# Taking GpSimd arithmetic out of the mixers and merges, and reordering the first expert search, in a two-layer hybrid network

## The chip, the cores and the metric

One core of one Trainium2 chip runs the whole network in one launch. The metric is the time of one execution on the device in microseconds. The engines are TensorE (PE; its weight loads are PEld), VectorE (DVE), ScalarE (ACT), GpSimd (POOL) and SyncE (SP). They run side by side, and each works through its own queue of instructions in order.

## The reference, cut to what matters

Two layers act on 512 latent rows (`x_lat`) and 256 context rows (`x_ctx`) of width 1024:

```python
for l in range(DEPTH):
    h_lat = rmsnorm(x_lat, norm1_g[l]) * (1.0 + sc1) + sh1          # same for h_ctx
    ys = ssm_mixer(...)      # two diagonal complex state-space scans (forward, backward), 16 groups
    yd = diff_mixer(...)     # differential attention, 4 heads
    yn = na_mixer(...)       # neighbourhood attention, 4 heads
    m = sigmoid(g_ssm)*(ys@w_br_ssm) + sigmoid(g_diff)*(yd@w_br_diff) + sigmoid(g_na)*(yn@w_br_na)
    x_lat = x_lat + g1 * (m @ w_out[l])
    x_lat = x_lat + g2 * peer_ffn(h2, peer_wq[l], peer_subkeys[l], peer_u[l], peer_v[l])
    # context rows: the same in layer 0, left out after the mixers' inputs in layer 1

def peer_ffn(h, ...):        # 8 heads, 128 x 128 = 16384 experts, 16 chosen for each row and head
    s = einsum(h @ wq, subkeys); sv, si = top_k(s, 16)        # twice, one for each half of the key
    best, pos = top_k(sv0[:, None] + sv1[None, :], 16); eidx = ...
    act = gelu(einsum(u_tab[eidx], h)); return einsum(softmax(best) * act, v_tab[eidx])
```

All is fp32; the kernel splits the operands of its large products into a high and a low part (`hi`, `lo`) and sums three products.

## The kernel before, in words

`run` calls `layer` twice. A layer has three stages.

`front`: the inputs are normalised (`start`, in layer 0), then three streams are woven together: `mixers` (projections and attention), `states` (`ssm_prep` and `ssm`) and `gates`. `ssm_prep` computes the tables of the state-space scans: complex powers, the matrices `sbt`, `scb` and the rotations `rot`. In layer 0 it runs beside `start`; the tables of layer 1 are prepared at the end of layer 0's `states`. `ssm` scans two groups at a time. All complex products go through `cmul` (L236): four instructions on VectorE, and on GpSimd the product at L243 and, unless `neg` is set, the sum at L247.

`merge` (L926) runs for the context rows and for the latent rows in layer 0, for the latent rows in layer 1. For each of 8 slices of 128 columns it takes three products, weighs each with its gate on VectorE (L946), sums the three on GpSimd (L947, L948), and splits the sum into `mh` and `ml` (ScalarE L61, VectorE L62). Then the output product, times a gate on VectorE (L968), is added to the rows on GpSimd (L969). In layer 0 `modulation` for layer 1 is woven in beside it; both stream weights through a ring of three `raw` buffers.

The expert stage: `own` rows (the context rows in layer 0, 128 latent rows in layer 1) are computed by gathering the chosen rows of `u` and `v`; the others by running all experts densely. `routing` holds in layer 0: `chosen` for the context rows (the search: queries, scores, `top16`), `route` for each of the two tiles (which writes the row numbers, `picks`), then the search and routes of the latent rows (`rest`), woven with `counted` at 1.0 to 0.9. `counted` steps through `gathered`: one indirect DMA of 128 rows on GpSimd's queue (L1200, five ahead) and one VectorE instruction (L1214 or L1222). `early` is 128 dense units: each splits a block of 512 KB and takes 24 products with the 512 latent rows. After both, `experts` takes the second dense product, with what is left of the gathers beside it.

What sets the order is `weave` (L123): a stream yields a cost for each step, and the stream with the smallest share of its total goes next. The totals are written out by hand. The framework then places the instructions on each engine's queue, and can move one ahead of another where the data allow it. All loads and most stores go through SP's queue.

Of the kernel before, what the change touches and what calls it, by code (L numbers as in the profile page):

```python
# [50 lines left out]
class Net:  # L51
# [87 lines left out]
    def drain(g):  # L139
        for _ in g:  # L140
            pass

    @contextmanager
    def psum(self, **banks):

        with ExitStack() as es:
            self.banks = {k: n if isinstance(n, str) else es.enter_context(
                self.tc.tile_pool(name=k, bufs=n, space=PSUM, reuse_waits="tile")) for k, n in banks.items()}
            yield
# [85 lines left out]

    def cmul(self, o, x, y, t, neg=False):  # L236

        v, g = self.nc.vector, self.nc.gpsimd
        v.tensor_mul(o[0], x[0], y[0])
        v.tensor_mul(t, x[1], y[1])  # L240
        v.tensor_sub(o[0], o[0], t)
        v.tensor_mul(t, x[0], y[1])
        g.tensor_mul(o[1], x[1], y[0])  # L243
        if neg:
            v.scalar_tensor_tensor(o[1], o[1], -1.0, t, op0=ALU.mult, op1=ALU.subtract)
        else:
            g.tensor_add(o[1], o[1], t)  # L247

    def exps(self, x, p, name, shape):

# [675 lines left out]
    def merge(self, l, x, t0, n, p):  # L926

        nc, v = self.nc, self.nc.vector
        ts = slice(t0, t0 + n)
        yh, yl, mh, ml = [p.tile([128, 8, n], F32R, name=a, bufs=1) for a in ("yh", "yl", "mh", "ml")]  # L930
        for k in range(8):
            t = p.tile([128, n], F32, name="yt")
            self.dma(t, self.ybuf[l][k, :, ts])
            self.split(t, yh[:, k], yl[:, k])
            yield 0.50
        for j in range(4):
            w = self.wchunk(self.a["w_br"][l, j])
            for h in range(2):
                c = slice(128 * h, 128 * h + 128)
                g = p.tile([128, 3, n], F32, name="g3")  # L940
                self.dma(g, self.gbuf[l][2 * j + h, :, :, ts])
                for b, (k0, nk) in enumerate(((0, 2), (2, 4), (6, 2))):
                    ps = self.ps1("mg")
                    self.mm3(ps[:, :n], lambda k: (w[0][:, k0 + k, c], w[1][:, k0 + k, c]),
                             lambda k: (yh[:, k0 + k], yl[:, k0 + k]), nk)
                    v.scalar_tensor_tensor(g[:, b], g[:, b], 1.0, ps[:, :n], op0=ALU.add, op1=ALU.mult)  # L946
                nc.gpsimd.tensor_add(g[:, 0], g[:, 0], g[:, 1])  # L947
                nc.gpsimd.tensor_add(g[:, 0], g[:, 0], g[:, 2])  # L948
                self.split(g[:, 0], mh[:, 2 * j + h], ml[:, 2 * j + h])
            yield 5.00  # L950
        tiles = range(t0 // 128, (t0 + n) // 128)
        gate = {}
        for r in sorted({1 if i < 2 else 0 for i in tiles}):
            gate[r] = p.tile([128, D], F32, name=f"g1{r}", bufs=1)
            self.dma(gate[r], self.arow[l][r:r + 1, 2 * D:3 * D].to_broadcast([128, D]))
        xt = {}
        for i in tiles:
            xt[i] = p.tile([128, D], F32, name=f"x{i - tiles[0]}", bufs=1)
            self.dma(xt[i], x[i])
        for j in range(4):  # L960
            w = self.wchunk(self.a["w_out"][l, j])
            c = slice(256 * j, 256 * j + 256)
            for i in reversed(tiles):
                t = slice(128 * i - t0, 128 * i - t0 + 128)
                ps = self.ps1("mg")
                self.mm3(ps[:, :256], lambda k: (mh[:, k, t], ml[:, k, t]), lambda k: (w[0][:, k], w[1][:, k]), 8)
                d = p.tile([128, 256], F32, name="d")
                v.scalar_tensor_tensor(d, ps[:, :256], 0.5, gate[1 if i < 2 else 0][:, c], op0=ALU.mult, op1=ALU.mult)  # L968
                nc.gpsimd.tensor_add(xt[i][:, c], xt[i][:, c], d)  # L969
            yield 4.00  # L970
        for i in reversed(tiles):
            self.dma(self.xs[i], xt[i])
# [409 lines left out]
    def layer(self, l):  # L1382
        self.front(l)
        own = (0, 1) if l == 0 else (2,)
        n = 512 if l == 0 else 384
        with self.pool("ga", 1, "right") as pa:
            rows = {i: pa.tile([128, D], F32, name=f"row{i}") for i in own}
            picks = {i: (pa.tile([128, 128], U32, name=f"pick{i}"), pa.tile([128, 128], F32, name=f"pw{i}")) for i in own}
            sums = self.gathered(l, own, rows, picks, pa)
            left = [256.0 * len(own)]  # L1390

            def counted():
                for c in sums:
                    left[0] -= c
                    yield c

            self.pace = None

            def routing():
                got = []  # L1400
                if l == 0:
                    with self.pool("route", 2) as p:
                        hc = [p.tile([128, 8, 256], F32R, name=a, bufs=1) for a in ("hch", "hcl")]
                        with self.pool("fin") as pn:
                            self.prepared(l, 0, hc, 0, rows, p, pn)
                        yield 5.0
                        yield from self.chosen(l, 0, 256, hc, got, p)
                        for i in own:
                            yield from self.route(l, *got[i], p, picks=picks[i])
                    got = []  # L1410
                with self.pool("route", 2) as p:
                    def rest():
                        if l == 0:
                            yield from self.chosen(l, 0, 512, h2, got, p)
                        for i in range(2, 6):
                            if i not in own:
                                yield from self.route(l, *got[i - 2], p, at=4 * (i - 2))

                    if l > 0:
                        yield from self.chosen(l, 0, 512, h2, got, p)  # L1420
                        for i in own:
                            yield from self.route(l, *got[i - 2], p, picks=picks[i])
                    yield from self.weave((rest(), 1.0), (counted(), GATHER[l]), lead=True)

            with self.pool("h2", 1, "right") as ph, self.stream(ROWS, 4), self.psum(mm=4, s=4), self.pool("early", 2) as pe:
                h2 = [ph.tile([128, 8, 512], F32R, name=a) for a in ("h2h", "h2l")]
                with self.pool("norm", 1) as p, self.pool("fin") as pn:
                    for i in (2, 4):
                        self.prepared(l, i, h2, 128 * (i - 2), rows, p, pn)
                self.drain(self.weave((routing(), 760.0 if l == 0 else 420.0), (self.early(l, h2, n, pe), 128.0)))  # L1430

            self.gate = {}
            late = [(i, rows[i]) for i in own]
            with self.psum(stay=n // 128), self.stream(ROWS, 2, LAST + 3), self.pool("ep", 2) as pe:
                def beside():
                    yield from counted()
                    for i in own:
                        self.finish(l, i, rows[i], rows[i])
                        yield 5.0

                def ends(x, acc):
                    i = 6 - n // 128 + x
                    to = pe.tile([128, D], F32, name=f"sum{x}", bufs=1)
                    self.finish(l, i, acc, to)
                    if l < DEPTH - 1:
                        late.append((i, to))

                        while late and (x == n // 128 - 1 or x and len(late) > 1):
                            self.renew(l, *late.pop(0))

                self.experts(l, n, pe, ends, beside(), left[0] + 5.0 * len(own))
# [103 lines left out]
```

## Time and profile before

| | |
|---|---|
| median of 3 runs | 4922.6 us (4914.19 to 4927.8) |
| profiled execution | 4922.7 us, span 4920.9 us |
| mean granted TensorE clock | 0.95 |
| busy: TensorE / VectorE / ScalarE / GpSimd | 91% / 76% / 38% / 28% |
| mixers of layer 0, then merge | to about 800 us, to about 1095 us |
| expert stage of layer 0 | about 1140 to 2900 us, the first gather at 1284.88 us |
| layer 1 | from about 2900 us |

Busy time is the time in which an engine executes something. The granted clock is the share of full speed that TensorE had in a stretch. "Idle before" names the instruction whose end let the waiting one go.

### The profile page before, as it was taken

To read this page: it belongs to the slowest core of one execution; us is meant where nothing else is said; L and a number is where in the kernel's file an instruction comes from. 1 tells how busy PE (TensorE), PEld (TensorE's weight loads), DVE (VectorE), ACT (ScalarE), POOL (GpSimd) and SP (SyncE) were. 2 spreads that over 40 slices of the span, in tenths; PEclk is the share of its full clock that TensorE was granted. 3 is DMA by queue.
4 is the path that set the end of the run, shared out by engine and by line. 5 is a ranking of instruction groups with operands and counts; after the bars stand their busy time and mean duration, and the time that the engine had idled before them with its cause. 6 is when DMAs were issued, how large, how long until landed. Compare 5 with 4: busy or idle time off the path is not lost. (4 is left out here: it accounts for less than half of the span.)

```text
span 4920.9 us, 69116 instructions
## 1 busy us (share of the span) xinstructions
PE 4470.1 (91%) x24197; PEld 3733.3 (76%) x24197; DVE 3763.9 (76%) x8444; ACT 1845.4 (38%) x3019; POOL 1371.3 (28%) x1088
## 2 busy tenths in 40 slices
PE   7898898888998899887999997999769999989998
PEld 3687776677776787666888886877669999978887
DVE  8277885646888899997878854877545799978888
ACT  3144344424322254442222223445233355533333
POOL 4000210120265445643333310000200033334552
PEclk8999899898999999998999998999889999999999
DMA  5553434754598789999999965542434489999997
GB/s 203 168 149 101 133 123 131 238 187 148 200 329 315 265 315 341 340 333 373 367 341 345 347 213 173 149 131 94 162 124 138 156 324 350 342 331 386 367 378 269
DMA packets 462839, 1215.19 MB, mean 247 GB/s; under 512 B 47690, under 2 KB 181914, under 8 KB 458906
## 3 DMA queue, kind: packets, MB, share of 16 engines
q1 hardware_dynamic: 311002, 690.61, 41.3%
q0 software_dynamic: 110592, 402.70, 22.4%
q10 hardware_dynamic: 40896, 117.46, 6.1%
q8 instruction: 190, 3.11, 0.3%
q14 instruction: 159, 1.30, 0.1%
HBM read 1031.54 MB, written 179.04 MB: 246 GB/s over the span
## 5 line engine op out<-in xcount | busy, mean ns | idle before, releaser
L1200 POOL DMA_INDIRECT grow<-in_u_rows,pick x384 | 519.5, 1353 | 1223.8 <-DVE grow L1214 381.1
L61 ACT CAST hi<-raw 128x1024 fp32r<-128x1024 f32 x490 | 512.4, 1051 | 899.6 <-PE s L71 589.7
L62 DVE TENSOR_TENSOR lo<-raw,hi 128x1024 fp32r<-128x1024 f32 x490 | 606.6, 1241 | 314.2 <-ACT hi L61 307.6
L72 PE MATMUL s<-h2h,lo 128*128 128x512 f32 (+1 forms) x2048 | 764.7, 374 | 62.0 <-DVE lo L62 61.7
L1200 POOL DMA_INDIRECT grow<-in_v_rows,pick x384 | 608.2, 1584 | 695.5 <-PE stay L1271 236.2
L70 PE MATMUL s<-h2h,hi 128*128 128x512 f32 (+1 forms) x2048 | 773.0, 378 | 12.9 <-ACT eact L1238 8.3
L71 PE MATMUL s<-h2l,hi 128*128 128x512 f32 (+1 forms) x2048 | 761.2, 372 | 0.2 <-DVE h2l L62 0.2
L1268 PE MATMUL stay<-hiv,wh 128*128 128x512 f32 x1792 | 708.5, 396 | 46.9 <-ACT hiv L61 46.9
L1269 PE MATMUL stay<-lov,wh 128*128 128x512 f32 x1792 | 708.4, 395 | 0.0
L1271 PE MATMUL stay<-hiv,wl 128*128 128x512 f32 x1792 | 562.6, 395 | 0.0
L1222 DVE SCALAR_TENSOR_TENSOR row<-grow,gw,row 128x1024 f32<-128x1024 f32 x381 | 488.0, 1281 | 94.3 <-DMA grow<-in_v_rows,pick 91.6
L1214 DVE SCALAR_TENSOR_TENSOR grow<-grow,row 128x1024 f32<-128x1024 f32 x384 | 463.2, 1220 | 98.3 <-DMA grow<-in_u_rows,pick 97.7
L72 PEld LDWEIGHTS s<-h2h,lo 128*128 128x128 f32 x2048 | 391.7, 191 | 121.4 <-DVE lo L62 76.3
L61 ACT CAST wh<-w 128x512 fp32r<-128x512 f32 (+1 forms) x256 | 145.3, 568 | 784.4 <-DVE w L1258 379.6
L70 PEld LDWEIGHTS s<-h2h,hi 128*128 128x128 f32 x2048 | 392.7, 192 | 60.9 <-ACT eact L1238 13.4
L1268 PEld LDWEIGHTS stay<-hiv,wh 128*128 128x128 f32 x1792 | 338.4, 189 | 126.0 <-ACT hiv L61 47.4
L71 PEld LDWEIGHTS s<-h2l,hi 128*128 128x128 f32 x2048 | 391.7, 191 | 44.7 <-DVE h2l L62 0.6
L1269 PEld LDWEIGHTS stay<-lov,wh 128*128 128x128 f32 x1792 | 338.4, 189 | 80.2 <-DVE lov L62 1.3
L1271 PEld LDWEIGHTS stay<-hiv,wl 128*128 128x128 f32 x1792 | 338.1, 189 | 78.9
L62 DVE TENSOR_TENSOR lov<-raw,hiv 128x1024 fp32r<-128x1024 f32 x256 | 312.1, 1219 | 5.2 <-ACT hiv L61 4.9
L61 ACT CAST hiv<-raw 128x1024 fp32r<-128x1024 f32 x256 | 268.0, 1048 | 57.1 <-DMA raw<-in_peer_v 53.4
L1258 DVE TENSOR_TENSOR w<-act,gt 128x512 f32<-128x512 f32 (+1 forms) x256 | 158.8, 621 | 105.2 <-DMA act<-actd 103.7
(431 smaller groups left out, 8963.2 us busy)
## 6 DMA issues: line engine op xcount, KB each, us to landing
raw<-in_peer_u SPq DMA_DIRECT2D x256, 512.0 KB
raw<-in_peer_v SPq DMA_DIRECT2D x256, 512.0 KB
gd<-gst ACTq DMA_DIRECT2D x28, 2048.0 KB
raw<-in_w_in SPq DMA_DIRECT2D x88, 512.0 KB
actd<-eact ACTq DMA_DIRECT2D x128, 256.0 KB
gt<-gd SPq DMA_DIRECT2D x16, 2048.0 KB
act<-actd SPq DMA_DIRECT2D x128, 256.0 KB
adaw<-in_ada_w SPq DMA_DIRECT2D x48, 512.0 KB
```

Of the source, the lines that this page charges most:

```text
L61: self.nc.scalar.copy(hi, x)
L62: self.nc.vector.tensor_sub(lo, x, hi.bitcast(F32))
L70: mm(ps, lh, rh, start=start and k == 0, stop=False)
L71: mm(ps, lh, rl, start=False, stop=False)
L72: mm(ps, ll, rh, start=False, stop=stop and k == n - 1)
L1200: d = nc.gpsimd.indirect_dma_start(out=t, out_offset=None, in_=self.a[table], in_offset=bass.IndirectOffsetOnAxis(ap=picks[y][0][:, j:j + ...
L1214: v.scalar_tensor_tensor(t, t, 1.0, h, op0=ALU.mult, op1=ALU.mult, accum_out=u[:, j:j + 1])
L1222: v.scalar_tensor_tensor(h, t, w[:, j:j + 1], h, op0=ALU.mult, op1=ALU.add)
L1258: v.tensor_mul(w.rearrange("p (b t) -> p b t", t=32), act.rearrange("p (b t) -> p b t", t=32), self.gt[:, :, i % 8])
L1268: nc.tensor.matmul(ps[:, c], wh[:, t], vh[:, c], start=i == 0, stop=False)
L1269: nc.tensor.matmul(ps[:, c], wh[:, t], vl[:, c], start=False, stop=False)
L1271: m = nc.tensor.matmul(ps[:, c], wl[:, t], vh[:, c], start=False, stop=i == 127)
```

## The change

Complex products and the additions in the merge are issued on VectorE. In the merge each gated product is added as soon as it is there, instead of both additions after the third. In the first layer the search for the context rows is wrapped in `at(0.4, ...)`, which multiplies every cost that it yields, and the total of `routing` becomes 730 in place of 760.

```diff
+    @staticmethod
+    def at(price, g):
+        for c in g:
+            yield price * c
...
     def cmul(self, o, x, y, t, neg=False):
-        v, g = self.nc.vector, self.nc.gpsimd
+        v = self.nc.vector
...
-        g.tensor_mul(o[1], x[1], y[0])
+        v.tensor_mul(o[1], x[1], y[0])
         if neg:
             v.scalar_tensor_tensor(o[1], o[1], -1.0, t, op0=ALU.mult, op1=ALU.subtract)
         else:
-            g.tensor_add(o[1], o[1], t)
+            v.tensor_add(o[1], o[1], t)
...
                     v.scalar_tensor_tensor(g[:, b], g[:, b], 1.0, ps[:, :n], op0=ALU.add, op1=ALU.mult)
-                nc.gpsimd.tensor_add(g[:, 0], g[:, 0], g[:, 1])
-                nc.gpsimd.tensor_add(g[:, 0], g[:, 0], g[:, 2])
+                    if b:
+                        v.tensor_add(g[:, 0], g[:, 0], g[:, b])
...
-                nc.gpsimd.tensor_add(xt[i][:, c], xt[i][:, c], d)
+                v.tensor_add(xt[i][:, c], xt[i][:, c], d)
...
-                        yield from self.chosen(l, 0, 256, hc, got, p)
+                        yield from self.at(0.4, self.chosen(l, 0, 256, hc, got, p))
...
-                self.drain(self.weave((routing(), 760.0 if l == 0 else 420.0), (self.early(l, h2, n, pe), 128.0)))
+                self.drain(self.weave((routing(), 730.0 if l == 0 else 420.0), (self.early(l, h2, n, pe), 128.0)))
```

## Rows read from the trace of the kernel before

**Rows 1.** The page, busy time of each engine, share of the span, instructions.

```profile
PE 4470.1 (91%) x24197; PEld 3733.3 (76%) x24197; DVE 3763.9 (76%) x8444; ACT 1845.4 (38%) x3019; POOL 1371.3 (28%) x1088
```

**Rows 2.** Stretches: busy us and count by engine, granted clock, DMA share, GB/s.

```profile
20.00:140.00 120.00, 104.71 (x534) 51.03 (x533) 102.84 (x338) 29.88 (x66) 57.73 (x90) 0.86 0.57 191
480.00:660.00 180.00, 149.83 (x895) 127.51 (x895) 154.80 (x529) 59.73 (x143) 52.49 (x94) 0.90 0.37 122
968.00:1036.00 68.00, 59.03 (x287) 44.01 (x285) 43.81 (x50) 25.53 (x39) 25.28 (x15) 0.92 0.74 257
1146.00:1256.00 110.00, 110.00 (x689) 97.92 (x688) 70.24 (x264) 46.39 (x72) 0.00 (x0) 1.00 0.48 152
1260.00:1320.00 60.00, 49.79 (x198) 38.78 (x198) 59.60 (x220) 17.86 (x23) 7.45 (x7) 0.91 0.42 146
1320.00:1700.00 380.00, 338.32 (x1444) 271.36 (x1443) 327.10 (x935) 97.82 (x146) 207.63 (x148) 0.94 0.86 309
1700.00:2220.00 520.00, 475.55 (x2707) 375.71 (x2707) 508.17 (x895) 239.53 (x282) 275.94 (x167) 0.97 0.90 328
2260.00:2900.00 640.00, 640.00 (x2756) 518.85 (x2755) 512.00 (x601) 182.92 (x233) 235.58 (x185) 1.00 0.97 352
3488.00:3541.00 53.00, 45.17 (x194) 36.67 (x193) 31.44 (x39) 12.88 (x16) 22.36 (x15) 0.92 0.57 189
```

**Rows 3.** Waits in the whole span: who waited for whom, total us, times, longest.

```profile
ACT mh L61 <- POOL g L948: 83.4, 23, 6.0
DVE rt L240 <- POOL rot L247: 8.4, 24, 0.7
```

**Rows 4.** VectorE's groups by shape: count, busy us, mean ns, idle before.

```profile
L240 DVE TENSOR_TENSOR st<-sx,rot_l 128x192 f32<-128x192 f32 x16 | 10.1, 629 | 0.0
L242 DVE TENSOR_TENSOR st<-sx,rot_l 128x192 f32<-128x192 f32 x16 | 5.6, 351 | 0.1
L239 DVE TENSOR_TENSOR big<-s,s 128x512 f32<-128x512 f32 x16 | 10.9, 683 | 0.5 <-PE sm L423 0.5
L240 DVE TENSOR_TENSOR rt<-rot,s 128x128 f32<-128x128 f32 x16 | 7.2, 447 | 4.3 <-POOL rot L247 4.3
L239 DVE TENSOR_TENSOR rot<-rot,s 128x128 f32<-128x128 f32 x16 | 4.1, 281 | 0.0
L968 DVE SCALAR_TENSOR_TENSOR d<-mg,g 128x256 f32<-128x256 f32 x40 | 16.9, 423 | 64.4 <-PE mg L72 63.2 <-POOL x L969 1.2
```

**Rows 5.** GpSimd's groups by shape, columns as above.

```profile
L243 POOL TENSOR_TENSOR sz<-sx,rot_l 128x192 f32<-128x192 f32 x16 | 10.6, 662 | 572.2 <-DVE sx L587 261.4 <-DMA raw<-in_w_in 220.1 <-ACT ah L61 34.3
```

**Rows 6.** Timeline, last step of layer 1's merge: start us, duration us, instruction, idle before.

```profile
3535.93 1.22 DVE L62 TENSOR_TENSOR lo<-raw,hi 128x1024 fp32r<-128x1024 f32 x1
3537.07 1.28 DVE L946 SCALAR_TENSOR_TENSOR g<-g,mg 128x512 f32<-128x512 f32 x2
3538.26 1.96 DVE L62 TENSOR_TENSOR lo<-raw,hi 128x1024 fp32r<-128x1024 f32 x1
3539.22 2.12 POOL L948 TENSOR_TENSOR g<-g 128x512 f32<-128x512 f32 x1
3541.37 0.62 ACT L61 CAST mh<-g 128x512 fp32r<-128x512 f32 x1 [5.87 <-POOL g L948]
3542.05 0.58 PE L70 MATMUL mg<-hi,mh 128*128 128x256 f32 x1 [7.27 <-ACT mh L61]
```

**Rows 7.** TensorE's groups from 1146 to 1256 us: count, busy us, mean ns.

```profile
L72 PE MATMUL s<-h2h,lo 128*128 128x512 f32 x82 | 32.8, 400 | 0.0
```

**Rows 8.** Timeline, TensorE: two dense products, then two of the search.

```profile
1178.30 0.40 PE L71 MATMUL s<-h2l,hi 128*128 128x512 f32 x1
1178.53 0.40 PE L72 MATMUL s<-h2h,lo 128*128 128x512 f32 x1
1178.77 0.28 PE L70 MATMUL mm<-hch,hi 128*128 128x256 f32 x1
1178.89 0.28 PE L71 MATMUL mm<-hcl,hi 128*128 128x256 f32 x1
```

## The prediction, made before the changed kernel ran

> **What bounds the kernel now.** I read the page's shares first: TensorE is busy 91% of the span, VectorE 76%, GpSimd 28% [rows 1]. These shares are averages, so the busy time by stretch comes next [rows 2]; the reader is to look in it for the engine whose busy time fills the stretch. From 2260 to 2900 us (the experts of the first layer) it is TensorE, 640.00 of 640 us at full clock: nothing that the change does to other engines counts there. From 1146 to 1256 us (the search for the context rows, with dense units woven in) it is TensorE again, 110.00 of 110, while VectorE has 40 us free. From 1260 to 1320 us (the routes after that search) it is VectorE, 59.60 of 60. From 1320 to 1700 us nobody is full: TensorE 338 and VectorE 327 of 380, the DMA engines 0.86. From 1700 to 2220 us it is VectorE, 508 of 520. In 20 to 140 us and 480 to 660 us, where the two state-space preparations run, VectorE is busy 102.84 of 120 and 154.80 of 180. In the merge (968 to 1036 us) no engine is full: TensorE 59 of 68.
>
> Then the waits on GpSimd [rows 3]: ScalarE's cast of the merged gate waits 83.4 us in 23 waits for the second GpSimd addition, and VectorE waits 8.4 us in all for the rotation products. GpSimd arithmetic is thus not a bottleneck by its busy time; it sits in chains, and most visibly in the merges.
>
> **Change 1: the complex product moves to VectorE.** In `cmul` two instructions move, the product of L243 and, where `neg` is off, the sum of L247. By the calls in the code that is 122 products and 106 sums. I price them by VectorE rows of the same shape [rows 4]: 32 of 128x512 at 0.683 us = 21.9 us; 32 of 128x128 at 0.281 = 9.0; 32 of 128x192 at 0.351 = 11.2; the other 132, of 4 to 256 elements, at an estimated 0.18 (the 0.281 us of 128 elements is their upper neighbour) = 24. Gross 66 us more on VectorE.
>
> Against it stands what GpSimd costs VectorE now. The same 128x192 product takes 0.629 us on the mean at L240, where the GpSimd product of 0.662 us [rows 5] runs beside it, and 0.351 at L242, where none does: 16 x 0.278 = 4.4 us. The 128x128 pair gives 16 x (0.447 - 0.281) = 2.7. With the 8.4 us of waiting that is 15.5 us shown. I take twice that, 31, as an estimate: some hundred smaller operations have the same neighbours, and unrelated VectorE work is stretched too (a `lo` of 1.96 us beside a GpSimd sum, against 1.22 [rows 6]). Net 35 us: about 15 for each preparation, 5 for the two scans. In a scan group GpSimd's product and sum leave the chain at about the time that VectorE now needs for them (0.28 us of stretch and some waiting against 2 x 0.351), so the scans cost almost nothing.
>
> What hides the 15 us: the first preparation lies in 20 to 140 us, where VectorE has 17 us free, the second in 480 to 660 us with 25 us free [rows 2]. Both just fit, but each engine works through its queue in order, and a VectorE instruction that comes later holds the TensorE transposes and products behind it. I let a quarter of the net through: **+9 us**. Bounds: 0 (all in the gaps; a small gain is possible where the relief is larger) and +35 (none hidden), +66 if the relief were nothing.
>
> The Trainium skill (SBUF — State Buffer, Who interferes with whom) says that a VectorE instruction with two SBUF inputs and a GpSimd instruction that reads SBUF lock each other out for the whole instruction. The 0.629 against 0.351 us agrees in kind; by that rule the relief could reach GpSimd's 57.7 and 52.5 us of busy time in those two stretches, and this part would be free or a gain.
>
> **Change 2: the merges' additions move.** Three groups: 24 + 24 additions of the three gated products (L947, L948) and 40 of L969. On VectorE they cost 32 x 0.683 + 16 x 0.423 + 40 x 0.423 [rows 4] = 46 us, in stretches with a third of VectorE free [rows 2], so I price that at nothing by itself; should the cover fail, a `lo` split comes 0.68 us later and TensorE after it.
>
> The chain is what changes. In one step [rows 6] the last two products on VectorE start at 3537.07 and end at 3538.35; GpSimd's sums then run until 3541.34 and ScalarE's cast starts at 3541.37, 3.0 us after the last product. TensorE starts the output product at 3542.05 after 7.27 us of idling. With both additions on VectorE the cast starts two times 0.68 after that point: 1.6 us earlier. There are 16 steps of 512 columns and 8 of 256 (the latter at about half): 16 x 1.6 + 8 x 0.9 = 33 us of waiting taken from ScalarE, whose queue has the casts of the next weights behind it. What TensorE can win back is bounded by its idle time: 9 of 68 us in 968 to 1036 and 8 of 53 in 3488 to 3541, some 8 more by the same share in the 256-column steps, 25 us in all, and a little clock (0.92 granted in both [rows 2]). I take half of the 33: **-16 us**. Bounds: 0 (the weights' transfers are late anyway) and -33; an extra VectorE queue of 46 us uncovered is the other end, but a third of that engine is free there. What is late next is the weights' DMA behind three buffers. The last addition before the rows are stored is shorter too; I count it at nothing.
>
> **Change 3: the search goes ahead.** `at(0.4, ...)` lets the search for the context rows count 23.04 units in the weave in place of 57.6 (eight heads of 3.00 + 2 x 2.10), and the total is 730 in place of 760. Dense units woven into the search: before 57.6 x 128/760 = 9.7, after 23.04 x 128/730 = 4.0, so 5.7 fewer. The trace has 244 or so dense products in that stretch (82 on L72 [rows 7], three lines alike), 10.2 units. In this stretch TensorE is full, at a product every 0.23 us for the dense units and every 0.12 us for the search [rows 8]: a unit of 24 products is 5.5 us, 5.7 units are **-31 us**. Check: 10.2 x 5.5 + 384 x 0.12 + scores = 56 + 46 + 8 = 110. What is left is 79 us of TensorE against VectorE's 70.24 - 5.7 x 1.22 = 63 [rows 2, 6], so TensorE still sets it, with 16 us of room. Each head then comes every 10 us in place of 14. With the units go their 512 KB loads on SP's queue, their raw buffers and their stores on ScalarE's queue; the DMA share is 0.48 there, so the search's own loads are not squeezed. The first gather, now behind the first route, starts about 31 us earlier.
>
> The units are not gone. The first routes and their preparation take 0.3 more; the second search counts 115.2 x 1.9 = 219 in the weave (gathers at 0.9 beside it), so 36.9 units become 38.4: 1.5 more from 1320 to 1700 us, and the other 3.8 go to the table part. In the first TensorE is 89% busy and I charge it in full: 1.5 x 5.5 = 8. In the second VectorE is the full one and a unit costs it one `lo`, 1.22 us: 3.8 x 1.22 = 5. Together +13. Bounds: +7 (all at VectorE's price) and +29 (all at TensorE's). The same number of gather rows is consumed before the experts, since their ratio to the rest of the routing is untouched, and the experts are full of TensorE work. So this part is **-18 us**, between -24 and -2.
>
> **Sum.** The profiled execution took 4922.7 us (span 4920.9), the median of the runs 4922.6, so no correction between them. 4922.7 + 9 - 16 - 18 = 4897.7, forecast **4898 us**. A difference under 0.3% (15 us) is what a measurement of this kernel cannot tell from no change.
>
> **Rivals.** (a) Work is only moved. The dense units cost TensorE full price where they land (-31 + 29 = -2), and the merges' casts wait for weights instead (ScalarE already waits for transfers between casts), gain 4. With the preparations hidden: 4922.7 - 2 - 4 = 4917. For it: TensorE is 89 to 91% busy from 1320 to 2220 us [rows 2]. Against: VectorE, not TensorE, fills the last 520 of those us.
>
> (b) Slower: VectorE becomes the bound of the two preparations. Price 35 us net, all of it on the path, with the merges at 0 and the search at -8: 4922.7 + 35 - 8 = 4950. It decides from the point at which the net addition of a preparation passes the 17 us that VectorE has free in 20 to 140 us, that is, when the relief there is under about 10 of the gross 27 (half of 66 less the scans' 11). For it: that stretch is already 86% full. Against: the relief is seen in the rows. The Trainium skill (Perfetto Trace Analysis, Optimizing Scalar/DVE Operations) speaks for it in part: work may be handed from a saturated VectorE even to GpSimd, and the change goes the other way; the same section adds that sharing a read port may spoil that, which the 0.629 us agrees with.
>
> (c) All of it counts: search -24, merges -33, preparations 0: 4866. For it: ScalarE's queue holds the casts for everything in the merges. Against: TensorE's idle time there is only 25 us.
>
> (d) The search doesn't come out shorter, because with fewer dense units TensorE idles between a head's product, copy and score, and its clock falls: in the routes TensorE runs 49.79 of 60 us with 0.91 granted [rows 2]. If 15 of the 31 us are lost so: 4913. This is counted with (a).
>
> **How the numbers follow.** Forecast 0.45, (a) with (d) 0.27, (b) 0.13, (c) 0.15. Faster by over 0.3% are the forecast and (c): 0.60. Within 0.3%: (a) and (d), 0.27. Slower: (b), 0.13. The range goes from 4868, where (c) is reached, to 4932, halfway to (b); under a tenth lies beyond either end.
>
> **What would show it.** Right: GpSimd's busy time falls to the gathers; the product of L240 drops to 0.35 us; ScalarE's wait before the merged cast halves; the first gather starts near 1255 us less what the merges have gained; some 5 dense units lie before the end of the first search. Wrong: VectorE over 97% in 20 to 140 us with TensorE waiting behind it; TensorE idle in the first search; the distance from first gather to the first expert product grown by 25 us or more.

## The result, and the profile after

The changed kernel took 4840.5 us at the median (4828.1 to 4844.4, 4 runs) against 4921.5: a ratio of 0.9832 [0.9809, 0.9854]. It gained 81 us where 24 were forecast, and 4840 lies below the range. The first fence is the page's busy line of the changed kernel.

```profile
PE 4437.8 (92%) x24197; PEld 3718.5 (77%) x24197; DVE 3786.0 (78%) x8760; ACT 1849.3 (38%) x3019; POOL 1130.1 (23%) x772
```

Beside [rows 1]: VectorE has 316 instructions more and is busy only 22 us more. GpSimd has just its gathers left.

Where the time went is seen best between landmarks. The next two fences give the stretch from 20 us to the first product of the scans (`sz`), and from there to the start of the merge (`yh`); first before, then after.

```profile
20.00:281.20 261.20, 233.99 (x1384) 155.85 (x1383) 136.09 (x410) 66.27 (x140) 58.63 (x92) 0.91 0.51 169
281.20:802.70 521.50, 474.06 (x3042) 406.88 (x3040) 427.73 (x1408) 229.24 (x581) 65.53 (x114) 0.96 0.38 116
```

```profile
20.00:261.60 241.60, 223.38 (x1384) 152.85 (x1383) 136.32 (x500) 66.42 (x140) 0.00 (x0) 0.95 0.55 182
261.60:762.50 500.90, 468.96 (x3053) 404.94 (x3053) 425.00 (x1523) 229.62 (x581) 0.00 (x0) 0.97 0.39 121
```

Columns after the length are TensorE, its loads, VectorE, ScalarE, GpSimd, granted clock, DMA share, GB/s. Each stretch is 20 us shorter, 40 in all. VectorE does 90 and 115 more instructions in them in the same busy time: 136.09 against 136.32, 427.73 against 425.00. TensorE is busy 10.6 and 5.1 us less in them, at a granted clock of 0.95 against 0.91 and of 0.97 against 0.96.

| landmark, first start in us | before | after | gained so far |
|---|---|---|---|
| first scan product `sz` | 281.2 | 261.6 | 20 |
| merge of layer 0 `yh` | 802.7 | 762.5 | 40 |
| search `hch` | 1146.5 | 1091.3 | 55 |
| first gather `grow` | 1284.9 | 1201.8 | 83 |
| first expert product `stay` | 2247.0 | 2173.0 | 74 |
| layer 1 `hn` | 2957.4 | 2883.7 | 74 |
| span | 4920.9 | 4837.2 | 84 |

So the mixers of layer 0 gave 40 us (forecast: a loss of 9), the merge of layer 0 15, the search 28 with 9 given back behind it, and layer 1 10. The lines that answer to [rows 2] are these: the start, a stretch of layer 1's merge, and the search.

```profile
20.00:140.00 120.00, 112.17 (x616) 55.33 (x614) 104.48 (x437) 32.54 (x75) 0.00 (x0) 0.96 0.68 228
3407.00:3460.00 53.00, 49.35 (x221) 40.33 (x221) 38.92 (x56) 14.15 (x18) 0.00 (x0) 0.91 0.65 222
1091.30:1168.30 77.00, 77.00 (x547) 72.08 (x546) 57.85 (x242) 36.53 (x58) 0.00 (x0) 1.00 0.50 158
```

To [rows 3] answers ScalarE's wait for the merged gate:

```profile
ACT mh L61 <- DVE g L954: 30.7, 16, 4.3
```

To [rows 4], VectorE's groups by shape:

```profile
L246 DVE TENSOR_TENSOR st<-sx,rot_l 128x192 f32<-128x192 f32 x16 | 5.6, 351 | 0.0
L249 DVE TENSOR_TENSOR sz<-sx,rot_l 128x192 f32<-128x192 f32 x16 | 5.6, 352 | 0.0
L246 DVE TENSOR_TENSOR rt<-rot,s 128x128 f32<-128x128 f32 x16 | 4.5, 279 | 0.1
```

And to [rows 7], the dense products in the search, from 1091.3 to 1168.3 us:

```profile
L72 PE MATMUL s<-h2h,lo 128*128 128x512 f32 x36 | 14.3, 398 | 0.0
```

In 20 to 140 us TensorE is busy 112 us against 105, and VectorE, with 99 instructions more, 104.5 against 102.8. In the merge TensorE has 4 of 53 us more. The product of L246 (L240 before) takes 0.351 us in place of 0.629.

The last step of layer 1's merge answers to [rows 6]:

```profile
3456.82 1.88 DVE L952 SCALAR_TENSOR_TENSOR g<-g,mg 128x512 f32<-128x512 f32 x3
3458.62 0.68 DVE L954 TENSOR_TENSOR g<-g 128x512 f32<-128x512 f32 x1
3459.22 1.22 DVE L62 TENSOR_TENSOR lo<-raw,hi 128x1024 fp32r<-128x1024 f32 x1
3460.35 0.68 DVE L954 TENSOR_TENSOR g<-g 128x512 f32<-128x512 f32 x1
3461.07 0.62 ACT L61 CAST mh<-g 128x512 fp32r<-128x512 f32 x1 [4.30 <-DVE g L954]
3461.74 0.38 PE L70 MATMUL mg<-hi,mh 128*128 128x256 f32 x1 [1.89 <-ACT mh L61]
```

The cast starts 2.4 us after the last gated product's end (3458.70), against 3.0 before: a `lo` split has slid between the two sums. TensorE idles 1.89 us before the output product, not 7.27.

### The profile page after: what moved, and what is told of

Same layout as the page of the kernel before. It is cut to its first block, busy times and chain, and to the rows that moved or that the text cites. A ratio compares the mean times of both kernels' runs of the same rounds, so it can differ in the third digit from the quotient of the medians.

```text
span 4837.2 us, 68859 instructions
## 1 busy us (share of the span) xinstructions
PE 4437.8 (92%) x24197; PEld 3718.5 (77%) x24197; DVE 3786.0 (78%) x8760; ACT 1849.3 (38%) x3019; POOL 1130.1 (23%) x772
## 5 line engine op out<-in xcount | busy, mean ns | idle before, releaser
L62 DVE TENSOR_TENSOR lo<-raw,hi 128x1024 fp32r<-128x1024 f32 x490 | 595.5, 1218 | 290.5 <-ACT hi L61 287.2
L72 PE MATMUL s<-h2h,lo 128*128 128x512 f32 (+1 forms) x2048 | 762.4, 373 | 54.6 <-DVE lo L62 54.2
L72 PEld LDWEIGHTS s<-h2h,lo 128*128 128x128 f32 x2048 | 391.5, 191 | 112.1 <-DVE lo L62 66.7
```

Source lines behind the costliest of these rows:

```text
L62: self.nc.vector.tensor_sub(lo, x, hi.bitcast(F32))
L72: mm(ps, ll, rh, start=False, stop=stop and k == n - 1)
```

## The experiments

Each ratio is to the kernel before, run beside it (its medians lay between 4917.7 and 4924.1). "To changed" is the median less 4840.5; below some 10 us it means nothing. `e13_hop` and `e15_fill` leave a part of the computation out; the others compute all of it.

| run | median us | ratio to before | to changed |
|---|---|---|---|
| e1_cmul | 4878.6 | 0.9916 [0.9896, 0.9936] | |
| e2_merge | 4900.2 | 0.9959 [0.9943, 0.9975] | |
| e3_search | 4904.0 | 0.9968 [0.9955, 0.9981] | |
| e4_side | 4869.5 | 0.9912 [0.9880, 0.9944] | +29 |
| e5_double | 4863.0 | 0.9870 [0.9853, 0.9887] | +22 |
| e6_sum | 4852.4 | 0.9857 [0.9840, 0.9874] | +12 |
| e7_product | 4863.2 | 0.9871 [0.9854, 0.9889] | +23 |
| e8_scans | 4847.9 | 0.9845 [0.9822, 0.9867] | +7 |
| e9_ahead | 4850.5 | 0.9860 [0.9843, 0.9876] | +10 |
| e10_xadd | 4829.5 | 0.9818 [0.9802, 0.9834] | -11 |
| e11_order | 4835.8 | 0.9832 [0.9812, 0.9852] | -5 |
| e12_write | 4834.4 | 0.9825 [0.9809, 0.9842] | -6 |
| e13_hop | 4845.1 | 0.9839 [0.9816, 0.9862] | +5 |
| e14_mid | 4864.5 | 0.9877 [0.9853, 0.9900] | +24 |
| e15_fill | 4831.2 | 0.9814 [0.9798, 0.9830] | -9 |
| e16_total | 4839.7 | 0.9832 [0.9816, 0.9848] | -1 |
| e17_copy | 4872.5 | 0.9901 [0.9873, 0.9929] | +32 |

### Each part alone

`e1_cmul` is the kernel before with the six lines of `cmul`, `e2_merge` with the additions of the merge, `e3_search` with `at(0.4, ...)` and 730: the diff above, cut in three.

> Only the complex products (cmul) go to VectorE; merges and search stay as before. Theory A (most of what the prediction missed lies in the state-space preparations and the mixers of layer 0, where the milestones of the changed kernel come 40 us early): about 4880 us, 35 to 50 us under the kernel before, with layer 0's merge beginning near 762 us in place of 802. Rival B (the complex products cost what was predicted, +9, and the 40 us come from elsewhere, by another order of the instructions): 4915 to 4935 us.

> Only the merges' additions go to VectorE. Theory A: 20 to 26 us under the kernel before (15 in layer 0's merge, 9 in layer 1's), about 4898. The prediction's own term: -16, 4906. Rival B (the waits of ScalarE are covered by the weights' transfers): within 6 us of the kernel before.

> Only the search's price (0.4) and the total 730. Theory A: the search is 28 us shorter, 9 to 13 us come back in the rest of the routing, so 15 to 20 us under the kernel before, about 4904. Rival B (work is only moved): within 5 us of the kernel before.

The parts gain 43, 21 and 17 us: 81, the whole, so no action of one part on another shows beyond the noise of some 10 us. The merges and the search came out near their terms (16 and 18). The surprise is all in the complex products. By the page of `e1_cmul`, it isn't that VectorE has more or less to do:

```profile
PE 4452.4 (91%) x24197; PEld 3726.4 (76%) x24197; DVE 3761.8 (77%) x8672; ACT 1847.0 (38%) x3019; POOL 1232.7 (25%) x860
```

VectorE took over 228 instructions and is busy 2.1 us less than before (3763.9). In `e3_search` the first gather moves from 1284.9 to 1257.1 us.

### What GpSimd costs beside VectorE, and what VectorE's own work costs

`e4_side` is the changed kernel with GpSimd repeating the products into a tile that nobody reads; `e5_double` has VectorE repeat them.

```diff
         v.tensor_mul(o[1], x[1], y[0])
+        ...                                   # m: pieces of at most 256 elements; s: their scratch tile
+        for i in range(1 if neg else 2):
+            for k in range(0, sh[1], m):
+                self.nc.gpsimd.tensor_mul(s, x[1 - i][:, k:k + m], y[i][:, k:k + m])   # e5: v.tensor_mul
```

> The changed kernel, and beside each complex product GpSimd computes the same products again from the same inputs into a scratch tile that nobody reads: GpSimd is as busy in the mixers as before, but nobody waits for it, and the order on VectorE, TensorE and ScalarE is that of the changed kernel. Theory L (what went away is the stretching of VectorE's instructions beside GpSimd's): 25 us or more of the gain comes back, 4865 us or more, with the 128x192 product of L246 at 0.6 us again in place of 0.35. Rival C (what went away is the chain through GpSimd: its slower instructions and the waits for them): under 10 us come back, 4840 to 4850.

> The changed kernel, and VectorE computes the moved products a second time (two for each complex product, one where neg is set) into a scratch tile that nobody reads: about 70 us more of VectorE's own work in the mixers. The prediction's view (VectorE has 17 and 25 us free beside the preparations, a quarter of an addition gets through): about 15 to 20 us over the changed kernel, 4855 to 4860. Theory V (in the preparations a microsecond more of VectorE is almost a microsecond of the kernel, as the run with GpSimd's side products suggests, where 41 us more of VectorE's busy time cost 29 us): 45 to 65 us over it, 4885 to 4905.

Products whose results nobody waits for cost 29 us on GpSimd (39 by the ratio, which one run of 4892.9 us pulls) and 22 on VectorE. The fence shows two VectorE groups of `e4_side`, the next its two stretches.

```profile
L246 DVE TENSOR_TENSOR st<-sx,rot_l 128x192 f32<-128x192 f32 x16 | 9.2, 577 | 0.0
L249 DVE TENSOR_TENSOR sz<-sx,rot_l 128x192 f32<-128x192 f32 x16 | 8.8, 549 | 0.0
```

```profile
20.00:274.50 254.50, 226.84 (x1384) 153.86 (x1383) 151.94 (x502) 66.14 (x141) 75.07 (x109) 0.93 0.52 173
274.50:795.40 520.90, 473.97 (x3053) 408.37 (x3052) 445.06 (x1522) 229.69 (x582) 75.07 (x130) 0.96 0.38 117
```

The same products take 0.577 and 0.549 us in place of 0.351 and 0.352. The first stretch is 13 us longer than in the changed kernel, two thirds of the way back to the length of before, and the second 20 us, all the way. VectorE is busy 16 and 20 us more in them: the lengthening is its own. On the page of `e4_side` it is busy 3827.4 us, 41 more than in the changed kernel with the same instructions, for 29 us of time: 0.7 us for each (0.95 by the ratio). In `e5_double` 260 products more make it 3832.6, 47 us more, and each of these us costs 0.47: far from VectorE setting the pace. The 22 us are near what the prediction's way of counting gave, but by two errors that offset: 47 us of work came where some 70 were counted, and half of it got through where a quarter was allowed.

### One half back, the scans back

`e6_sum` puts the sum back on GpSimd, `e7_product` the product, `e8_scans` both, for the scans' rotation alone.

```diff
-        v.tensor_mul(o[1], x[1], y[0])
+        self.nc.gpsimd.tensor_mul(o[1], x[1], y[0])      # e7_product
...
-            v.tensor_add(o[1], o[1], t)
+            self.nc.gpsimd.tensor_add(o[1], o[1], t)     # e6_sum
```

> The changed kernel with the sums of the complex products alone back on GpSimd (106 instructions, 52 us of GpSimd in the kernel before), each of which waits for VectorE and is waited for. Theory C (the chain VectorE, GpSimd, VectorE is what the kernel before lost): 25 us or more of the 42 come back, 4865 or more. Rival L (only the stretching of VectorE beside GpSimd counts, and against it the sums' own 30 us that VectorE is spared): within 10 us of the changed kernel, 4830 to 4850.

> The changed kernel with the products alone back on GpSimd (122 instructions, 71 us of GpSimd in the kernel before); their result is not needed until three VectorE instructions later. Theory C: little comes back, under 15 us, 4835 to 4855. Rival L: as much as for the sums by GpSimd's time or more (some 60% of the whole): if that whole is the 42 us, 20 to 30 us come back, 4860 to 4870.

> The changed kernel with both instructions back on GpSimd in the scans alone (16 groups, 22 us of GpSimd), the preparations on VectorE. The prediction priced the scans at nothing: within 5 us of the changed kernel. Rival (the scans, on the path of the states stream, carry a part of the 42 us): 10 us or more over it.

12 and 23 us come back, 35 of the 43. The product costs more than the sum, as the rival had it; the chain theory had it the other way round (25 or more for the sum, under 15 for the product). The page of `e7_product`:

```profile
PE 4460.6 (92%) x24197; PEld 3729.7 (77%) x24197; DVE 3794.3 (78%) x8638; ACT 1848.1 (38%) x3019; POOL 1188.9 (24%) x894
```

VectorE is busy 3794.3 us: with 122 instructions fewer, 8 us more. That alone says that handing GpSimd these products spares VectorE nothing. The scans have some 7 us, inside the noise, so most of the cost is in the two preparations.

### Reading or merely running?

`e12_write` is `e4_side` with fills in place of the products.

```diff
-                self.nc.gpsimd.tensor_mul(s, x[1 - i][:, k:k + m], y[i][:, k:k + m])
+                for _ in range(3):
+                    self.nc.gpsimd.memset(s, 0.0)
```

> Changed kernel, with GpSimd doing extra work beside VectorE's complex products that only writes: three fills of an unread scratch tile in place of each product that the run e4_side added (that run was 29 us slower than the changed kernel). Order on VectorE, TensorE and ScalarE is that of the changed kernel. Theory (the cost comes from both engines reading SBUF, as the Trainium skill, SBUF - State Buffer, Who interferes with whom, has it): within 5 us of the changed kernel, and the 128x192 VectorE products stay near 0.35 us. Rival (any GpSimd work beside VectorE costs): 15 us or more slower, with the same products at 0.5 us or above.

No cost shows. First GpSimd's group, then the stretch up to the scans.

```profile
L260 POOL MEMSET scr<- 128x16 f32 (+5 forms) x780 | 158.5, 203 | 54.0 <-DVE row L1239 9.0 <-POOLq L1563 0.3
```

```profile
20.00:262.90 242.90, 222.97 (x1385) 152.39 (x1384) 138.22 (x501) 66.42 (x140) 131.91 (x642) 0.95 0.55 182
```

GpSimd works 158 us, as long as in `e4_side` (162 on its page's groups), 132 of it in this stretch, which is 242.9 us long against 241.6. The fills wait for no operand and ran ahead, so none lies beside the second preparation; for the first, where 75 us of reading cost 13 us, 132 us of writing cost 1.

### Is it the order of the queues?

`e11_order` computes `o[1]` before `o[0]` in `cmul`, all on VectorE.

```diff
+        v.tensor_mul(t, x[0], y[1])
+        v.tensor_mul(o[1], x[1], y[0])
+        ...                                  # the sum or the subtraction into o[1]
         v.tensor_mul(t, x[1], y[1])
         v.tensor_mul(o[0], x[0], y[0])
         v.tensor_sub(o[0], o[0], t)
```

> Changed kernel, with the six VectorE instructions of the complex product in another sequence (the product t = x1 y1 first and the product into o[0] second); the same work, all on VectorE. It is a control for what a mere change of instruction order is worth, since taking GpSimd out also reorders the engines' queues. Theory (GpSimd's presence is what costs): within 8 us of the changed kernel. Rival (the order of the queues makes the difference): 20 us or more away on either side.

No difference. `e4_side` points the same way: VectorE, TensorE and ScalarE issue the same instructions in the same order as in the changed kernel.

### GpSimd in VectorE's chain, without and with reading

`e13_hop` puts two fills of `o[1]` behind each sum, `e17_copy` two copies. `e15_fill` sets GpSimd back where it stood: two fills of `o[1]` take the place of the product, and two that of the sum.

```diff
             v.tensor_add(o[1], o[1], t)
+            for _ in range(2):
+                self.nc.gpsimd.memset(o[1], 0.0)             # e13_hop
+                self.nc.gpsimd.tensor_copy(o[1], o[1])       # e17_copy
```

> Changed kernel, with two GpSimd fills of o[1] put behind each sum of the complex product (106 places; the imaginary parts are thus zero where the code takes the sum, so part of the computation is left out). All products and sums stay on VectorE, and GpSimd reads nothing there; but whatever reads o[1] waits for GpSimd, as in the kernel before, by about the time that its sum took (two fills of 0.1 to 0.6 us). Theory (the rest of change 1's gain is that results no longer pass through GpSimd): 10 to 30 us slower than the changed kernel, nearly all of it before the merge of layer 0. Rival (such waits are hidden; the rest is something else): within 5 us.

> GpSimd stands where it stood in the kernel before, but only writes: in the complex product the product into o[1] and, where it is taken, the sum are each two GpSimd fills of o[1] (so that part of the computation is left out); VectorE is spared the 66 us that change 1 gave it, and what reads o[1] waits for GpSimd. Theory (the shared reads, stretching VectorE and GpSimd and with it the chain, are what change 1 took away): no slower than the changed kernel; spared VectorE work gives 10 to 20 us (22 for 70 in e5_double), the waits take 5 to 15 (e13_hop), so between 15 us faster and 3 slower, about 4830. Rival (work handed to GpSimd is late whatever it reads): most of the 35 to 42 us come back, 20 us or more slower than the changed kernel.

> Changed kernel with two GpSimd copies of o[1] onto itself behind each sum of the complex product: e13_hop with copies, which read, in place of fills, which don't; all of VectorE's work stays. e13_hop was 5 us slower than the changed kernel. Theory (a GpSimd step that reads and stands in VectorE's chain is held up by VectorE's own reads, and the chain with it): 20 to 45 us slower than the changed kernel, the copies lasting well over the fills (0.11 us for 128x4, 0.22 for 128x128, 0.58 for 128x512). Rival (the cost is only VectorE's stretching, by e4_side's rate some 10 us for about 60 us of GpSimd work, and the chain's 5): 10 to 15 us slower. Third: if the copies are no longer than fills and cost 5 us, reading from one input isn't what matters.

`e13_hop` fell on its rival's side: 5 us. It did lose 17 by the merge (762.5 to 779.8 us), as the theory said, but not in the end. `e15_fill` is not slower than the changed kernel (9 us faster, inside the noise): with GpSimd in its old place but not reading, nothing is lost. By its page

```profile
PE 4433.9 (92%) x24197; PEld 3716.1 (77%) x24197; DVE 3755.6 (78%) x8532; ACT 1852.9 (38%) x3019; POOL 1203.4 (25%) x1228
```

VectorE is busy 30.4 us less than in the changed kernel, with 228 instructions fewer. `e17_copy` costs 32 us, 27 more than `e13_hop`, and VectorE, TensorE and ScalarE issue the same instructions in the same order in both. The next fences compare GpSimd's largest group and VectorE's largest wait for GpSimd, each in `e13_hop` and then in `e17_copy`; the last is `e17_copy`'s timeline (start, duration).

```profile
L255 POOL MEMSET rot<- 128x128 f32 (+5 forms) x112 | 17.1, 152 | 200.7 <-DVE rot L253 193.4 <-DVE nb L789 4.1
```

```profile
L255 POOL COPY rot<-rot 128x128 f32<-128x128 f32 (+5 forms) x112 | 48.8, 436 | 185.7 <-DVE rot L253 161.1 <-DVE e1z L795 9.0 <-DVE orst L520 8.3
```

```profile
DVE rt L246 <- POOL rot L255: 5.3, 15, 0.4
```

```profile
DVE rt L246 <- POOL rot L255: 13.3, 29, 0.8
```

```profile
103.44 7.74 POOL L255 COPY rot<-rot 128x128 f32<-128x128 f32 x4 [2.00 <-DVE rot L253]
...
136.74 0.64 POOL L255 COPY rot<-rot 128x128 f32<-128x128 f32 x2 [0.54 <-DVE rot L253]
```

Two copies of 128x128 take 0.64 us at one place and four take 7.74 at another, the first alone 6.80; on the mean over the six sizes of this group a copy lasts 436 ns, a fill 152. All the copies last 97.9 us and all the fills 43.0. A copy is also longer by itself (128x128: 0.29 us at the shortest, a fill 0.20); were each copy as short as the shortest of its size, they would last 58 us, so 40 us are time in which they are held up. The wait shown grows by only 8 us, and VectorE is busy 7.4 us more on the page (3800.0 against 3792.6 us in `e13_hop`). Even if each of these counts in full, some 20 of the 27 us are left for steps in the chain that last longer themselves.

### The merges' last additions, and the pace of the search

`e10_xadd` puts only L975's additions back on GpSimd. `e9_ahead` has 0.1 and 715 in place of 0.4 and 730, `e16_total` 0.4 and 760, and `e14_mid` is `e10_xadd` with 0.7 and 745.

```diff
-                        yield from self.at(0.4, self.chosen(l, 0, 256, hc, got, p))
+                        yield from self.at(0.1, self.chosen(l, 0, 256, hc, got, p))    # e14: 0.7; e16: 0.4
...
-                self.drain(self.weave((routing(), 730.0 if l == 0 else 420.0), ...
+                self.drain(self.weave((routing(), 715.0 if l == 0 else 420.0), ...     # e14: 745; e16: 760
```

> Changed kernel, with only the additions to x at the end of the merges (forty of 128x256) back on GpSimd; the sums of the three gated products stay on VectorE. Theory (the merges' gain lies in the chain product, sums, cast, output product; the x additions have nobody behind them until the rows are stored): within 5 us of the changed kernel. Rival (a GpSimd addition costs wherever it stands, by the same stretching as in the complex products): 8 us or more slower.

> Change 3 taken further: the search counts 0.1 in place of 0.4 and the total is 715 in place of 730, so about 3 more dense units leave the first search. Theory (a unit costs the search 5.5 us of TensorE and costs less where it lands): TensorE alone would give back 17 us, but VectorE, with some 60 us of work in the search, then becomes its limit; the units cost 4 to 8 us where they land. So 5 to 12 us faster than the changed kernel, about 4832. Rival (the search is already at VectorE's pace, or the units cost as much later): within 4 us of the changed kernel.

> e10_xadd (x additions on GpSimd) with the search's count at 0.7 and the total at 745, halfway back to the kernel before. 5.7 fewer dense units in the search gained 17 us (e3_search) and three more of them lost 10 to 14 (e9_ahead). Theory (the best point is near 0.4): 3 to 10 us slower than e10_xadd, about 4836. Rival (the loss of e9_ahead is the start of a slope that begins at a smaller shift, since VectorE's waits for gathered rows grow with it): 5 us or more faster than e10_xadd.

> Changed kernel with the weave's total at 760 as before, the search still counting 0.4: dense units go slower through all of the routing (0.168 a unit of cost in place of 0.175). Theory (the 0.4 alone makes the gain, the total only decides how much of it is given back in the routes and tables): the first search 1 to 2 us shorter, and within 6 us of the changed kernel. Rival (the total balances the queues: without it dense units pile up behind the routing, or the gathers and units get out of step as in e9_ahead and e14_mid): 10 us or more slower.

The forty additions to x cost nothing on GpSimd: `e10_xadd` has the lowest median, but its interval overlaps that of the changed kernel. The total is worth nothing either. `e9_ahead` missed: the search did lose 16 us (60.9 in place of 77.0), but from the first gather to the first expert product it took 993 us in place of 971. VectorE waits longer in that stretch for gathered rows; the changed kernel's line first.

```profile
DVE row L1228 <- DMA grow<-in_v_rows,pick: 19.1, 21, 4.0
```

```profile
DVE row L1228 <- DMA grow<-in_v_rows,pick: 34.2, 29, 4.3
```

That is 15 of the 22 us. `e14_mid` lost 35 us against `e10_xadd` (29 by the ratios), more than undoing change 3 whole (17), which neither side expected. From `hch` to the first gather it takes 127.2 us where `e10_xadd` takes 110.6 and the kernel before 138.4, which is near halfway. From there to the first expert product it takes 977.9 us against 963.0, where fewer units left over should have made it shorter. I can't explain these 15 us; no count of units gives them. No complete kernel here is measurably faster than the changed one.

## Why the prediction was wrong, point by point

**The step that failed** is change 1's term: "Gross 66 us more on VectorE", "Net 35 us", "I let a quarter of the net through: +9 us". It measured -43.

First, the gross was priced too high. I multiplied counts by durations: the 228 instructions last 65.6 us in the changed kernel, summed. But neighbours on VectorE overlap at their ends: products of 0.27 us start 0.20 apart. Counted from each start to the next instruction's start, or to the end where that comes first, they take 50.6 us; `e15_fill`, without them, is busy only 30.4 us less. Why it isn't 50 is not shown.

```profile
88.74 0.27 DVE L246 TENSOR_TENSOR rt<-rot,s 128x128 f32<-128x128 f32 x1
88.94 0.27 DVE L249 TENSOR_TENSOR rot<-rot,s 128x128 f32<-128x128 f32 x1
89.14 0.27 DVE L247 TENSOR_TENSOR rot<-rot,rt 128x128 f32<-128x128 f32 x1
```

Second, the relief. I took 31 us for it. As the net is -2.1 us by the page of `e1_cmul`, the relief was 2.1 us more than the gross, between 33 and 53 us. The net was thus -2, not 35.

Third, and largest: time was lost where I had no term, in GpSimd's own steps. I saw 8.4 us of VectorE waiting for GpSimd [rows 3] and took that for the chain's whole price. The next fence is the stretch from 20 us to the merge, before and after.

```profile
20.00:802.70 782.70, 708.05 (x4424) 562.73 (x4422) 563.82 (x1817) 295.51 (x721) 124.16 (x206) 0.95 0.42 134
20.00:762.50 742.50, 692.35 (x4435) 557.79 (x4434) 561.32 (x2022) 296.04 (x721) 0.00 (x0) 0.97 0.45 141
```

VectorE is busy 563.8 us of 782.7 before and 561.3 of 742.5 after. So 38 of the 40 us are idle time of VectorE, 218.9 us against 181.2, spread over many waits. The same stretch in other runs:

| run | length, us | VectorE busy | VectorE idle |
|---|---|---|---|
| changed kernel | 742.5 | 561.3 | 181.2 |
| before | 782.7 | 563.8 | 218.9 |
| e4_side | 775.4 | 597.0 | 178.4 |
| e6_sum | 754.9 | 556.9 | 198.0 |
| e7_product | 763.7 | 566.9 | 196.8 |
| e13_hop | 759.8 | 566.8 | 193.0 |
| e15_fill | 726.5 | 528.7 | 197.8 |
| e17_copy | 781.1 | 574.5 | 206.6 |

Where GpSimd reads and nobody waits for it (`e4_side`), VectorE's busy time grows and its idle time doesn't. Where its results are waited for, the idle time grows: by 17 us for the sums, 16 for the products, 38 for both. The sums cost less of the total because VectorE is busy 4 us less where GpSimd takes them, and 6 us more where it takes the products.

Both engines are held up, and what waits is not only the next reader. The trace of before shows it at 95 to 104 us:

```profile
95.76 2.27 DVE L62 TENSOR_TENSOR hl<-xt,hh 128x2048 fp32r<-128x2048 f32 x1
95.90 2.81 POOL L243 TENSOR_TENSOR rot<-rot,s 128x4 f32<-128x4 f32 x1 [5.23 <-DVE rot L239]
97.96 0.67 DVE L239 TENSOR_TENSOR big<-s,s 128x512 f32<-128x512 f32 x1
...
98.66 1.95 POOL L243 TENSOR_TENSOR big<-s,s 128x512 f32<-128x512 f32 x1
...
99.57 1.06 DVE L241 TENSOR_TENSOR rot<-rot,rt 128x4 f32<-128x4 f32 x1
...
102.49 0.20 POOL L243 TENSOR_TENSOR rot<-rot,s 128x8 f32<-128x8 f32 x1
102.60 0.15 DVE L240 TENSOR_TENSOR rt<-rot,s 128x8 f32<-128x8 f32 x1
102.66 3.93 POOL L243 TENSOR_TENSOR scb_s<-s,s 128x512 f32<-128x512 f32 x1
```

A GpSimd product of four elements lasts 2.81 us beside a VectorE split of 2.27 and the product behind it, where one of eight takes 0.20 seven us later. Then a VectorE subtraction of four elements lasts 1.06 us, until the GpSimd product beside it ends, where a product of eight takes 0.15. VectorE works in order, so all behind it is late too. In the rows this showed only as long instructions, not as waits.

So the balance of -43 is nearly all idle time of VectorE: its busy time changed by only -2.1 us (`e1_cmul`). That steps of GpSimd which read cost time in a chain is shown by `e17_copy` beside `e13_hop` (some 20 us for the 106 sums' places; change 1 took 122 products away too). How the 43 us divide further is argued: GpSimd in the chain adds 17 us of idle time in `e15_fill` without reading, which the work that VectorE is spared more than makes up for there, and TensorE's granted clock rose from 0.95 to 0.97 in the stretch.

The whole of it hangs on reading. With reading in GpSimd's old place the kernel would be 43 us slower, if the parts add (`e1_cmul`); with writing alone it is no slower (`e15_fill`). That pair alone does not show that it is the reading and not the length: the fills also last less (60 us of GpSimd in the first two stretches against 124) and those for the product wait for no operand. `e12_write` against `e4_side` has no such difference in length, though its fills too wait for no operand. The Trainium skill (SBUF — State Buffer, Who interferes with whom) says that a VectorE instruction with two SBUF inputs contends with a GpSimd instruction that reads SBUF and not with one that only writes it. The 158 us of fills in `e12_write` cost nothing that shows, as it says. In the prediction I had from that page that "this part would be free or a gain", and let the row of the 0.629 us outweigh it.

**Change 2**, -16: measured -21 (`e2_merge`). The mechanism was right: ScalarE's wait fell from 83.4 to 30.7 us, TensorE's idling before the output product from 7.27 to 1.89 in the step shown. A detail was wrong: in that step the cast came 0.6 us earlier, not 1.6, since the second sum now queues behind a split. The last additions count nothing, as said (`e10_xadd`).

**Change 3**, -18: measured -17 (`e3_search`). The search fell from 105.2 to 77.0 us (forecast 31 less), with 36 dense products on L72 left of 76 in that span, 4.5 units. 9 us came back behind it in the changed kernel (forecast 13). TensorE stayed full in the search, as expected: 77.00 of 77.

**The rivals.** (b) asked for VectorE as the bound of the preparations. It is 87% busy in 20 to 140 us, and more work on it does cost (22 us in `e5_double`), but the change brought none in net. (c), with the preparations at nothing, came nearest and was still 26 us too slow. (a) and (d) fell with `e3_search`.

## What to carry to other kernels

Before work is shared between VectorE and GpSimd, look at the same shape with and without a GpSimd neighbour, on both engines: where 0.35 us becomes 0.63 on one and 0.20 becomes 2.81 on the other, the sharing may spare VectorE nothing and hold up both queues. Price moved VectorE instructions by the spacing of their starts in a run of them (51 us here), not by their durations (66). A small sum of waits for an engine does not bound its price: long instructions and idle time elsewhere hide the rest. Compare the busy and idle time of the stretch, and run the kernel with that engine's work replaced by fills.

## What was not expected of the hardware

GpSimd's work beside VectorE's two-input instructions spared VectorE no time at all: 3763.9 us with 228 instructions on GpSimd, 3761.8 with them on VectorE. GpSimd writing without reading showed no cost: 132 us of fills beside the first preparation made that stretch 1.3 us longer. A GpSimd copy of 128x128, 0.29 us at the shortest, was once held up for 6.80 us.
